# Streaming the split weights of `mm3` through TensorE from the last column to the first

## The chip, the cores and the metric

The kernel runs on one core of a Trainium2 chip. The metric is the device time of one execution in microseconds. The kernel before took 1279.71 us (median of two runs, 1278.69 and 1280.73).

## What is computed

Two blocks, one after the other, on x of 256 tokens by 1024 channels, all in float32. The first has a state space layer (S5) and an attention layer; the second has two layers, each with a mixing part of three branches (latent attention, convolution, retention) and a gated feed-forward part. Nearly all of the arithmetic is products of the activations with weight matrices of 1024 rows or so:

```python
def second_block(x, ...):
    for l in range(DEPTH):                       # DEPTH = 2, D_MODEL = 1024, SEQ = 256
        h = rms_norm_2(x, ln_mix_pre[l])
        proj = h @ w_in[l]                       # 1024 x 7584
        ...
        merged = gates[:, :, 0] * y_mla + gates[:, :, 1] * y_conv + gates[:, :, 2] * y_ret
        x = x + rms_norm_2(merged @ w_out[l], ln_mix_post[l])
        h = rms_norm_2(x, ln_ffn_pre[l])
        f = (jax.nn.silu(h @ ffn_w_gate[l]) * (h @ ffn_w_up[l])) @ ffn_w_down[l]
        x = x + rms_norm_2(f, ln_ffn_post[l])
    return x
```

## The kernel before, in words

Activations are held transposed, 128 channels of 256 tokens a block, and weights are streamed. A float32 operand is split into two of the type float32r, hi and lo, with hi + lo the operand; a product is then three matmuls, hi by hi, hi by lo and lo by hi, added up in one accumulator in PSUM.

`wtile` (L142) brings one tile of weights: SyncE's queue issues the DMA to `raw` (L149), 256 rows by 512 columns as 128 partitions of 2 x 512; ScalarE copies it to `hi` (L158, rounding it), VectorE subtracts to get `lo` (L160). Each of raw, hi and lo has four buffers in turn, and hi and lo two more from the second layer on, so how far loads and splits run ahead depends on when TensorE is done with a tile.

`mm3` (L163) issues the three matmuls of one accumulator and one block of 128 rows, L165, L166 and L167. The stationary operand is a block of the activations, 128 channels by 128 tokens, and the moving one is 128 rows of the tile of weights, as many columns as the tile has. [...] Nobody else calls these lines: `gemm` (L169) goes over the rows of a weight matrix two blocks of 128 at a time, and for each over the two halves of the tokens; `out_rows` (L241) does the same over 1024 output columns and adds the residual. What `gemm` has accumulated is read by the caller's `evac`, on ScalarE or VectorE. Between two tiles `pump` issues smaller work that is queued up: transposes, attention heads, taps of the convolution.

Other products don't go through `mm3`. `gemm_t` (L439; its matmuls are L454 to L456) has the weights stationary and 256 tokens moving, split as above. `gemm_raw` (L415; L428) does the same on float32 operands that are not split. Both serve the first layer, ahead of 165 us. Transposes (L203 and others) are matmuls by a unit matrix.

Each engine's instructions stand in the order in which the code issues them, which for the queued work is where `pump` takes it; semaphore waits are put in by the language's own tracking of tiles.

Of the kernel before, what the change touches and what calls it, by code (L numbers as in the profile page):

```python
# [9 lines left out]
F32 = mybir.dt.float32  # L10
# [5 lines left out]
PSUM = bass.MemoryType.PSUM  # L16
# [7 lines left out]
C = 512  # L24
# [26 lines left out]
class Net:  # L51
# [16 lines left out]
    def stage(self, pages, temps, raws=0, halves=0):  # L68
        """pages and temporaries of a stage; what an earlier stage had is given back."""
        if getattr(self, "ctx0", None):  # L70
            self.ctx0.close()
        self.ctx0 = ExitStack()
        self.temps = temps
        self.wn, self.more = {}, {"raw": raws, "hi": halves, "lo": halves}
        self.bp = self.ctx0.enter_context(self.tc.tile_pool(name=self.nm("bp"), bufs=pages))
        self.sp = self.ctx0.enter_context(self.tc.tile_pool(name=self.nm("sp"), bufs=2))
# [8 lines left out]
    def page(self, shape, name, dt=F32):  # L85
        """up to 4 KB of each partition"""
        assert int(np.prod(shape[1:])) <= 1024, shape
        return self.bp.tile(shape, dt, tag="q4", name=self.nm(name))
# [46 lines left out]
    def wbuf(self, tag):  # L135
        """buffer of a tile of weights; the stage may have some more of them"""
        i = self.wn[tag] = self.wn.get(tag, -1) + 1
        more = self.more.get(tag, 0)
        pool, bufs = (self.wp, 4) if i % (4 + more) < 4 else (self.sp, more)
        return pool.tile([128, KT, C], F32 if tag == "raw" else F32R, tag=tag, name=self.nm(tag), bufs=bufs)  # L140
# [22 lines left out]
    def mm3(self, out, xh, xl, wh, wl, first, last):  # L163
        nc = self.nc
        nc.tensor.matmul(out, xh, wh, start=first, stop=False)  # L165
        nc.tensor.matmul(out, xh, wl, start=False, stop=False)  # L166
        nc.tensor.matmul(out, xl, wh, start=False, stop=last)  # L167

    def gemm(self, xs, W, c0, ncols, evac, pts=None):  # L169
        """rows: out[t] = x @ W[:, c0:c0+ncols]; xs: list over k blocks of (hi, lo) aps [128, 256]."""  # L170
        KB = len(xs)
        pts = [self.acc(), self.acc()]
        for k0 in range(0, KB, KT):
            kn = min(KT, KB - k0)
            hi, lo = self.wtile(W[k0 * 128:(k0 + kn) * 128, c0:c0 + ncols], kn, ncols)
            for t in range(2):
                for k in range(kn):
                    xh, xl = xs[k0 + k]
                    s = slice(t * 128, t * 128 + 128)
                    self.mm3(pts[t][:, :ncols], xh[:, s], xl[:, s], hi[:, k, :ncols], lo[:, k, :ncols],  # L180
                             k0 + k == 0, k0 + k == KB - 1)
            self.pump()
        for t in range(2):
            evac(t, pts[t][:, :ncols])

    def split(self, dh, dl, src, scale=None):
        """dh + dl = src * scale, src in PSUM."""
        nc = self.nc
        if scale is None:
            nc.scalar.activation(dh, src, AF.Copy)  # L190
            nc.vector.tensor_tensor(dl, src, dh.bitcast(F32), op=ALU.subtract)
        else:
            a = nc.scalar.activation(dh, src, AF.Copy if isinstance(scale, float) else AF.Identity, scale=scale)  # L193
            self.last_split = a, nc.vector.scalar_tensor_tensor(dl, src, scale, dh.bitcast(F32), op0=ALU.mult, op1=ALU.subtract)  # L194

    def transposed(self, t, row, pages, nb, gains=None, scale=None):
        """row [128 tok, nb*128] -> split blocks of pages, scaled per channel by gains."""
        nc = self.nc
        for b0 in range(0, nb, 4):
            bn = min(4, nb - b0)  # L200
            pt = self.small()
            for b in range(bn):
                nc.tensor.transpose(pt[:, b * 128:(b + 1) * 128], row[:, (b0 + b) * 128:(b0 + b + 1) * 128], self.ident)  # L203
            s = slice(t * 128, t * 128 + 128)
            dh, dl = pages[b0 // 4]
            if gains is None:
                self.split(dh[:, :bn, s], dl[:, :bn, s],
                           pt[:, :bn * 128].rearrange("p (b n) -> p b n", b=bn), scale)
            else:
                for b in range(bn):  # L210
                    self.split(dh[:, b, s], dl[:, b, s], pt[:, b * 128:(b + 1) * 128],
                               gains[:, b0 + b:b0 + b + 1])
# [28 lines left out]
    def out_rows(self, xs, W, x, post, out=None):  # L241
        """x + rms(xs @ W) * post, or x + xs @ W when post is None; the first 128 rows are done some tiles ahead."""
        nc = self.nc
        KB = len(xs)
# [47 lines left out]
    def rsqrt1(self, v):  # L292
        """-1024 / 27 / sqrt(v) of a column, by a step of third and one of second order."""
# [16 lines left out]
    # ------------------------------------------------------------------ consts  # L310
# [25 lines left out]
    def sincos(self, out_c, out_s, ang, tag, after=None):  # L336
        """sin and cos of ang (any size that float32 reduces), ang [128, ...]"""
# [18 lines left out]
    def tables2(self):  # L356
# [8 lines left out]
        self.cs = self.sp.tile([128, 2, 2, 80], F32, tag="cs", name="cs", bufs=1)  # (cos/sin, t, mla16|ret64)  # L365
# [5 lines left out]
        # log gammas: min(x, 0) - log1p(exp(-|x|)), log1p by the atanh series  # L371
# [20 lines left out]
        # distances: [m part, mt, n]: relu(n - m), relu(m - n)  # L392
# [9 lines left out]
    # ------------------------------------------------------------------ first block: state space layer  # L402
    def raw_tiles(self, W, c0, ncols, KB):
        """sources of the tiles of gemm_raw, in its order"""
        return [W[k0 * 128:(k0 + KT) * 128, c0 + n0:c0 + n0 + C] for k0 in range(0, KB, KT) for n0 in range(0, ncols, C)]

    def load_raw(self):
        """next tile of self.todo, in any of the buffers of a tile of weights"""
# [6 lines left out]
    def gemm_raw(self, xs, ncols, evac, after=None):  # L415
        """gemm_t on float32 operands that are not split, where the tensor engine has the time: a closure for each tile of self.pre."""
# [22 lines left out]
    def gemm_t(self, xs, W, c0, ncols, evac, order=None):  # L439
        """columns: out^T = W[:, c0:c0+ncols]^T x^T, evac(block, psum [128, 256]); order of the pairs of k blocks."""  # L440
# [20 lines left out]
    def s5_params(self, after):  # L461
# [10 lines left out]
        # powers of ab: [ri, pair, k], k = 0..4  # L472
# [18 lines left out]
        # one chunk further, on (re, -im): [[a, b], [-b, a]] of ab^4  # L491
# [5 lines left out]
        # f = (ab - 1) / (lr + i li)  # L497
# [15 lines left out]
        # sums for products in three multiplications  # L513
# [4 lines left out]
    def s5_bc(self):  # L518
# [4 lines left out]
        # B~ = f B  # L523
# [20 lines left out]
    def s5_pows(self):  # L544
        """powers 1..16 of ab^4: (-im, re, im), pair, power."""
# [19 lines left out]
    def cprod(self, eng, q, l0, Z, Zx):  # L565
        """ab^l z for pairs 8q..8q+7, l = l0..l0+3, as (k1, k2, k3): re = k1 + k3, im = k1 + k2."""
# [14 lines left out]
    def s5_w(self, q, eng):  # L581
        """pairs 8q..8q+7 of ab^k B~, k = 1..4, [(g2, p), qq, (q2, k, c)], pair = 2 qq + q2, re and im."""
# [7 lines left out]
    def s5_wt(self, W, q, w, after=None):  # L590
        """their lhsT [(q2, k, c), qq, (g2, p)]"""
# [8 lines left out]
    def s5_c(self, cab, q, eng):  # L600
        """pairs 8q..8q+7 of [(g2, p), pair, (l, c')] of C ab^l, l = 0..3, re and im."""
# [4 lines left out]
    def s5(self, x_in):  # L606
# [6 lines left out]
        # normalised input; gains go on its channels after the transposes  # L613
# [6 lines left out]
        # gains go on the channels of the input; 1 / rms on what comes out of the first product and on what goes into the second  # L620
# [47 lines left out]
        # block diagonal B~ (re, -im) and the zeros before the kernel taps  # L668
# [55 lines left out]
        # chunk inputs X = W u: [(g2, p), (re, -im), pair, 1 + j], replaced by the states after each chunk  # L724
# [14 lines left out]
        # scan over the 64 chunks: inside 4 groups of 16, across the groups, then what each group takes over  # L739
# [28 lines left out]
        # kernel taps K[l] = Re(C ab^l B~): [(q4, g2, c), pg, (l, c')], channels in order; spread to lower triangles  # L768
# [19 lines left out]
        # inside a chunk  # L788
# [58 lines left out]
        # gated linear unit, output  # L847
# [25 lines left out]
    # ------------------------------------------------------------------ second block: mixing  # L873
    def mix(self, l, x):
# [11 lines left out]
        # ---- gates, branch outputs, merge  # L886
# [31 lines left out]
    def conv(self, l, xs, W, hf):  # L918
        """a * sigmoid(gate), taps, layer norm over channels and silu; the taps are left to run beside what follows."""
# [80 lines left out]
    def rope_rows(self, o1, o2, x1, x2, c, s, tag):  # L1000
        """o1 = x1 c - x2 s, o2 = x2 c + x1 s"""
# [42 lines left out]
    def mla(self, l, parts):  # L1044
        """latent attention; its rows and heads are left to run beside what follows."""
# [102 lines left out]
    def retention(self, l, xs, W, rstd, half, gn):  # L1148
# [41 lines left out]
        def score(h):  # L1190
            """scores on their decay, D^T[m, n] = gamma_f^(n - m) or gamma_b^(m - n)"""
# [54 lines left out]
    # ------------------------------------------------------------------ first block: causal attention  # L1246
# [128 lines left out]
    # ------------------------------------------------------------------ ffn  # L1375
# [25 lines left out]
def _cols(a, w):  # L1401
    """[..., w*128] -> [128, n*w]: one column per block of 128 channels."""
# [68 lines left out]
```

## Time and profile before

| | |
|---|---|
| time, median of two runs | 1279.71 us |
| span of the profiled execution, first to last instruction | 1276.7 us |
| TensorE busy | 1235.7 us, 97% |
| VectorE busy | 948.3 us, 74% |
| ScalarE busy | 652.9 us, 51% |
| DMA | 210.6 MB, mean 165 GB/s |

The profiled execution's own time is given as its span alone, which lies 3.0 us below the median of the runs. Busy time is the time in which an engine had an instruction under way; matmuls overlap each other, so the distance of their starts and not their durations tells how fast they go. A line of a group names the tile that is written, an arrow, and the tiles that are read.

### The profile page before, as it was taken

To read this page: it belongs to the slowest core of one execution; us is meant where nothing else is said; L and a number is where in the kernel's file an instruction comes from. 1 tells how busy PE (TensorE), PEld (TensorE's weight loads), DVE (VectorE), ACT (ScalarE), POOL (GpSimd) and SP (SyncE) were. 2 spreads that over 40 slices of the span, in tenths; PEclk is the share of its full clock that TensorE was granted. 3 is DMA by queue.
4 is the path that set the end of the run, shared out by engine and by line. 5 is a ranking of instruction groups with operands and counts; after the bars stand their busy time and mean duration, and the time that the engine had idled before them with its cause. 6 is when DMAs were issued, how large, how long until landed. Compare 5 with 4: busy or idle time off the path is not lost.

```text
span 1276.7 us, 17877 instructions
## 1 busy us (share of the span) xinstructions
PE 1235.7 (97%) x6520; PEld 1029.5 (81%) x6520; DVE 948.3 (74%) x1923; ACT 652.9 (51%) x1073; POOL 51.8 (4%) x42
## 2 busy tenths in 40 slices
PE   7898799999999999999999999999999999999997
PEld 6787777787888888888788887888888887888886
DVE  6999489887889998857755555899998857755544
ACT  3112467675765544544644444666545445644432
POOL 3920000000000000000000000000000000000000
PEclk9779899999999999999999999999999999999999
DMA  9326656644454554555566564544554554665661
GB/s 319 83 43 99 166 174 209 192 136 137 142 164 138 161 161 152 164 201 179 189 180 184 171 235 151 175 134 147 166 159 153 179 184 148 218 190 161 193 211 50
DMA packets 125367, 210.60 MB, mean 165 GB/s; under 512 B 22112, under 2 KB 31328, under 8 KB 125280
## 3 DMA queue, kind: packets, MB, share of 16 engines
q1 hardware_dynamic: 117056, 204.24, 50.9%
q10 hardware_dynamic: 8224, 5.23, 2.1%
q8 instruction: 51, 0.84, 0.3%
q14 instruction: 36, 0.29, 0.1%
HBM read 205.83 MB, written 3.60 MB: 164 GB/s over the span
## 4 chain that ended last, share of the span: by engine, by line
PE 79%; DVE 13%; ACT 3%; DMA 3%; issue 2%; SPq 0%; DVEq 0%; ACTq 0%
PE mm L165 23%; PE mm L167 23%; PE mm L166 22%; DVE lo L160 2%; PE sm L203 2%; ACT hi L158 1%; PE sm L1119 1%; PE sm L1211 1%; DVE cacc L957 1%; PE sm L1094 1%; DVE s5pr L745 1%; PE sm L733 1%; DVE cm L586 1%; DVE s5pr L759 1%; PE mm L455 1%
## 5 line engine op out<-in xcount | busy, mean ns | idle before, releaser
L160 DVE TENSOR_TENSOR lo<-raw,hi 128x1024 fp32r<-128x1024 f32 (+2 forms) x372 | 440.1, 1186 | 235.8 <-ACT hi L158 234.4
L158 ACT ACTIVATE hi<-raw 128x1024 fp32r<-128x1024 f32 (+2 forms) x372 | 382.6, 1032 | 377.8 <-PE mm L167 290.4
L165 PE MATMUL mm<-hi,xTh 128*128 128x512 f32 (+2 forms) x1152 | 451.1, 394 | 1.6 <-ACT xTh L193 1.5
L167 PE MATMUL mm<-hi,xTl 128*128 128x512 f32 (+2 forms) x1152 | 443.7, 386 | 0.3 <-DVE t L297 0.2
L166 PE MATMUL mm<-lo,xTh 128*128 128x512 f32 (+2 forms) x1152 | 443.3, 385 | 0.2 <-DVE lo L160 0.2
L165 PEld LDWEIGHTS mm<-hi,xTh 128*128 128x128 f32 x1152 | 216.4, 188 | 48.9 <-ACT xTh L193 7.3
L167 PEld LDWEIGHTS mm<-hi,xTl 128*128 128x128 f32 x1152 | 216.3, 188 | 46.2 <-DVE t L297 1.5
L166 PEld LDWEIGHTS mm<-lo,xTh 128*128 128x128 f32 x1152 | 216.7, 188 | 41.2 <-DVE lo L160 0.5
L957 DVE SCALAR_TENSOR_TENSOR cacc<-aT,colp,cacc 128x256 f32<-128x256 f32 x240 | 104.2, 476 | 0.0
L165 PE MATMUL mm<-hi,fh 128*128 128x512 f32 x176 | 69.0, 392 | 0.0
L166 PE MATMUL mm<-lo,fh 128*128 128x512 f32 x176 | 68.9, 392 | 0.0
L167 PE MATMUL mm<-hi,fl 128*128 128x512 f32 x176 | 68.8, 391 | 0.0
L167 PEld LDWEIGHTS mm<-hi,fl 128*128 128x128 f32 x176 | 33.0, 187 | 7.4
L165 PEld LDWEIGHTS mm<-hi,fh 128*128 128x128 f32 x176 | 33.0, 188 | 7.3
L166 PEld LDWEIGHTS mm<-lo,fh 128*128 128x128 f32 x176 | 33.0, 188 | 7.2
L277 DVE SCALAR_TENSOR_TENSOR pg<-mm,post 128x512 f32<-128x512 f32 x16 | 11.0, 690 | 21.9 <-ACT pg L275 21.9
L194 DVE SCALAR_TENSOR_TENSOR xTl<-sm,colp,xTh 128x128 fp32r<-128x128 f32 x80 | 24.3, 345 | 3.5 <-ACT xTh L193 3.1
L454 PE MATMUL mm<-s5gh,hi 128*128 128x256 f32 x64 | 19.0, 305 | 7.1 <-ACT s5gh L844 7.1
L193 ACT ACTIVATE xTh<-sm,colp 128x128 fp32r<-128x128 f32 x80 | 24.4, 381 | 1.8 <-DVE xTl L194 1.7
L895 ACT ACTIVATE pg<-mm,t 128x512 f32<-128x512 f32 x24 | 16.5, 690 | 16.9 <-PE mm L167 16.9
L733 PE MATMUL sm<-s5U,s5W 64*64 64x64 f32 x256 | 21.2, 300 | 2.5 <-DMA s5U<-s5ud 2.5
L733 PEld LDWEIGHTS sm<-s5U,s5W 64*64 64x64 f32 x256 | 20.8, 207 | 3.2 <-issue 3.2
(387 smaller groups left out, 1513.2 us busy)
## 6 DMA issues: line engine op xcount, KB each, us to landing
raw<-in_w_in SPq DMA_DIRECT2D x112, 512.0 KB, 3.5
raw<-in_ffn_w_down SPq DMA_DIRECT2D x44, 512.0 KB, 3.8
raw<-in_ffn_w_gate SPq DMA_DIRECT2D x40, 512.0 KB, 3.7
raw<-in_ffn_w_up SPq DMA_DIRECT2D x40, 512.0 KB, 3.6
raw<-in_attn_w_in SPq DMA_DIRECT2D x32, 512.0 KB, 4.3
raw<-in_ret_w_o SPq DMA_DIRECT2D x16, 512.0 KB, 3.2
raw<-in_w_out SPq DMA_DIRECT2D x16, 512.0 KB, 3.2
raw<-in_ssm_w_glu SPq DMA_DIRECT2D x8, 512.0 KB, 4.9
```

The costliest lines, as they stand in the source:

```text
L158: nc.scalar.activation(h, r, AF.Copy)
L160: self.last_lo = nc.vector.tensor_tensor(l, r, h.bitcast(F32), op=ALU.subtract)
L165: nc.tensor.matmul(out, xh, wh, start=first, stop=False)
L166: nc.tensor.matmul(out, xh, wl, start=False, stop=False)
L167: nc.tensor.matmul(out, xl, wh, start=False, stop=last)
L193: a = nc.scalar.activation(dh, src, AF.Copy if isinstance(scale, float) else AF.Identity, scale=scale)
L194: self.last_split = a, nc.vector.scalar_tensor_tensor(dl, src, scale, dh.bitcast(F32), op0=ALU.mult, op1=ALU.subtract)
L203: nc.tensor.transpose(pt[:, b * 128:(b + 1) * 128], row[:, (b0 + b) * 128:(b0 + b + 1) * 128], self.ident)
L454: nc.tensor.matmul(o, wh, xh, start=first and b % 2 == 0, stop=False, skip_group_check=True)
L733: lx[q] = nc.tensor.matmul(pt[g * 64:g * 64 + 64, qq * 64:qq * 64 + 64], Wl[i][h][r, qq, g * 64:g * 64 + 64], U[r, 8 * h + qq, g, :], star ...
L895: nc.scalar.activation(gate[t, n], p, AF.Tanh, scale=hf(t))
L957: nc.vector.scalar_tensor_tensor(cacc[:, b, :], src, sc, cacc[:, b, :], op0=ALU.mult, op1=ALU.add)
```

## The change

In `mm3` three views are turned round in the free dimension: the output, and the hi and the lo half of the weights. A step of 1 from column 0 becomes a step of -1 from the last column. The activations, which are stationary, are as before. Docstrings and comments are taken out as well, without effect on the program; the matmuls' lines become L166, L167 and L168.

```diff
     def mm3(self, out, xh, xl, wh, wl, first, last):
         nc = self.nc
+        out, wh, wl = out[:, ::-1], wh[:, ::-1], wl[:, ::-1]
         nc.tensor.matmul(out, xh, wh, start=first, stop=False)
         nc.tensor.matmul(out, xh, wl, start=False, stop=False)
         nc.tensor.matmul(out, xl, wh, start=False, stop=last)
```

No instruction changes its place on any engine. What differs in the order is waits, 90 on TensorE and two on VectorE. On TensorE, in the attention layer's product, where `mm_2755` and `mm_2756` are the accumulators of the two halves of the tokens, `hi_2758` and `lo_2759` the tile of weights, `xTh_1802` and `xTl_1803` the activations, `sm_2521` and `sm_2552` the scores of two heads, and a name with _49 a semaphore of an engine, this stands before:

```order
L165 MATMUL mm_2755<-hi_2758,xTh_1802 128x512
L166 MATMUL mm_2755<-lo_2759,xTh_1802 128x512
L167 MATMUL mm_2755<-hi_2758,xTl_1803 128x512
L165 MATMUL mm_2756<-hi_2758,xTh_1802 128x512 [waits Activation_49]
L1303 MATMUL sm_2521<-akT_1886,aqT_1884 128x256 [waits Activation_49]
L1304 MATMUL sm_2521<-akT_1886,aqT_1884 128x128
L1303 MATMUL sm_2552<-akT_1886,aqT_1884 128x256 [waits PE_49]
```

And this on TensorE at the same place of the changed kernel:

```order
L166 MATMUL mm_2755<-hi_2758,xTh_1802 128x512
L167 MATMUL mm_2755<-lo_2759,xTh_1802 128x512
L168 MATMUL mm_2755<-hi_2758,xTl_1803 128x512
L166 MATMUL mm_2756<-hi_2758,xTh_1802 128x512 [waits PE_49,Activation_49]
L1304 MATMUL sm_2521<-akT_1886,aqT_1884 128x256 [waits Activation_49]
L1305 MATMUL sm_2521<-akT_1886,aqT_1884 128x128
L1304 MATMUL sm_2552<-akT_1886,aqT_1884 128x256
```

The wait on TensorE's own semaphore has gone from the second head's scores to the first matmul of the accumulator `mm_2756`. Over the whole program 52 matmuls of L165, each the first of an accumulator, have such a wait more, and 38 matmuls of other lines have one less. VectorE's split to lo loses a wait on TensorE at two tiles.

## Rows read from the trace of the kernel before

**Rows 1.** From the page: span, TensorE's busy share, its busy digits and granted clock in 40 slices, and the chain of work that ended last, by engine and by line.

```profile
span 1276.7 us, 17877 instructions
PE 1235.7 (97%) x6520; PEld 1029.5 (81%) x6520; DVE 948.3 (74%) x1923; ACT 652.9 (51%) x1073; POOL 51.8 (4%) x42
PE   7898799999999999999999999999999999999997
PEclk9779899999999999999999999999999999999999
PE 79%; DVE 13%; ACT 3%; DMA 3%; issue 2%; SPq 0%; DVEq 0%; ACTq 0%
PE mm L165 23%; PE mm L167 23%; PE mm L166 22%; DVE lo L160 2%; PE sm L203 2%; ACT hi L158 1%; PE sm L1119 1%; PE sm L1211 1%; DVE cacc L957 1%; PE sm L1094 1%; DVE s5pr L745 1%; PE sm L733 1%; DVE cm L586 1%; DVE s5pr L759 1%; PE mm L455 1%
```

**Rows 2.** Who waited for whom, in total, with the number of times and the longest: TensorE's longest and those of `mm3`, and the longest of the other engines' that bears on the weights.

```profile
PE mm L454 <- ACT s5gh L844: 7.1, 1, 7.1
PE sm L597 <- DVE cm L586: 6.4, 4, 3.2
PE sm L638 <- DMA first<-in_c_first: 5.0, 1, 5.0
...
PE mm L165 <- ACT xTh L193: 1.5, 6, 0.3
...
ACT hi L158 <- PE mm L167: 290.4, 194, 3.5
```

**Rows 3.** Groups of instructions of line L165, kept apart by shape (partitions x columns of the output): count, busy time in us, mean ns of one, idle time before them.

```profile
L165 PE MATMUL mm<-hi,xTh 128*128 128x512 f32 x1056 | 421.9, 401 | 1.1 <-ACT xTh L193 1.0
L165 PE MATMUL mm<-hi,fh 128*128 128x512 f32 x176 | 69.0, 392 | 0.0
L165 PE MATMUL mm<-hi,xTh 128*128 128x256 f32 x64 | 18.1, 284 | 0.0
L165 PE MATMUL mm<-hi,oTh 128*128 128x512 f32 x32 | 13.1, 410 | 0.0
L165 PE MATMUL mm<-hi,s5mh 128*128 128x512 f32 x32 | 12.8, 403 | 0.1
L165 PE MATMUL mm<-hi,cTh 128*128 128x512 f32 x32 | 12.7, 397 | 0.0
L165 PE MATMUL mm<-hi,xTh 128*128 128x416 f32 x32 | 11.6, 380 | 0.6 <-ACT xTh L193 0.5
L165 PE MATMUL mm<-hi,mcTh 128*128 128x512 f32 x16 | 6.3, 391 | 0.0
L165 PE MATMUL mm<-hi,mcTh 128*128 128x256 f32 x8 | 2.2, 279 | 0.0
```

**Rows 4.** TensorE's instructions in order of time from 839.7 us on: start in us, duration in us, line, output and operands.

```profile
839.71 0.39 PE L166 MATMUL mm<-lo,xTh 128*128 128x512 f32 x1
839.94 0.39 PE L167 MATMUL mm<-hi,xTl 128*128 128x512 f32 x1
840.17 0.39 PE L165 MATMUL mm<-hi,xTh 128*128 128x512 f32 x1
...
841.57 0.39 PE L165 MATMUL mm<-hi,xTh 128*128 128x512 f32 x1
841.80 0.39 PE L166 MATMUL mm<-lo,xTh 128*128 128x512 f32 x1
```

**Rows 5.** Busy time of each engine in three stretches, and behind POOL's the clock granted to TensorE, the DMA share and GB/s.

```profile
91.00:97.00 6.00, 6.00 (x29) 5.30 (x28) 6.00 (x23) 0.00 (x0) 4.28 (x1) 1.00 0.20 66
142.00:145.00 3.00, 3.00 (x16) 3.00 (x15) 0.00 (x0) 1.56 (x2) 0.00 (x0) 0.50 0.96 292
840.00:845.00 5.00, 5.00 (x23) 4.03 (x22) 5.00 (x17) 4.24 (x8) 0.00 (x0) 1.00 0.00 0
```

**Rows 6.** The waits of line L165 that take an instruction of their own in the weight-loading queue: durations in ns (least, median, longest), first and last start.

```profile
L165 PEldq EVENT_SEMAPHORE  x26: 51/51/51, 190.0 to 1028.1; - x26
```

**Rows 7.** TensorE in order of time from 142 us on, the matmuls of `gemm_t` on 256 columns.

```profile
142.05 0.41 PE L456 MATMUL mm<-s5gh,lo 128*128 128x256 f32 x1
142.27 0.41 PE L454 MATMUL mm<-s5gh,hi 128*128 128x256 f32 x1
142.48 0.41 PE L455 MATMUL mm<-s5gl,hi 128*128 128x256 f32 x1
142.69 0.41 PE L456 MATMUL mm<-s5gh,lo 128*128 128x256 f32 x1
```

**Rows 8.** TensorE in order of time from 92 us on, the matmuls of `gemm_raw`, runs of the same group merged: start of the first, time to the end of the last, count.

```profile
92.06 3.62 PE L428 MATMUL mm<-s5x,lo 128*128 128x256 f32 x16
95.51 3.62 PE L428 MATMUL mm<-s5x,raw 128*128 128x256 f32 x16
```

**Rows 9.** TensorE in order of time at 190 us, where `mm3` begins behind transposes.

```profile
190.34 0.49 PE L203 MATMUL sm<-first,x 128*128 128x128 f32 x3
190.60 0.47 PE L165 MATMUL mm<-hi,xTh 128*128 128x512 f32 x1
190.91 0.39 PE L166 MATMUL mm<-lo,xTh 128*128 128x512 f32 x1
```

## The prediction

> **What bounds the kernel now.** I read the page's busy times and clock line first, then its chain of work [rows 1]. TensorE is busy 97% of a 1276.7 us span, and from the sixth of 40 slices on the digits of its busy share are nines but for the last; those of its granted clock are nines from the sixth on. The chain that ended last is TensorE for 79%, and 68% of it is the three lines of `mm3`, L165 to L167. So the time of this kernel is, to first order, the number of columns that TensorE streams times the time for one.
>
> Second, the list of who waited for whom on TensorE [rows 2]: its longest waits are 7.1, 6.4 and 5.0 us, once or a few times each, on lines of the first block. Waits of `mm3` (L165) are 1.5 us together. The other way round, ScalarE's split of the weights (L158) waits 290 us for the last matmul of a tile (L167): the weights are ready before TensorE wants them, and the engines that make them wait for buffers. Nothing but TensorE's own pace is worth time behind `mm3`.
>
> Third, how many matmuls the change touches, from the groups kept apart by shape [rows 3]. L165 issues 1056 + 176 + 32 + 32 + 32 + 16 = 1344 of 512 columns, 64 + 8 = 72 of 256 and 32 of 416; L166 and L167 issue as many. That is 4032, 216 and 96: 4344 matmuls, 4032 x 512 + 216 x 256 + 96 x 416 = 2.160 million columns.
>
> Fourth, the pace of one. The durations of the groups (some 390 ns) overlap, so they are no price; the starts are. In a stretch of nothing but `mm3` ten starts, nine steps, lie within 2.09 us [rows 4], 232 ns for 512 columns, 0.454 ns each. [...] Each 10% on that price is 98 us: only this price matters.
>
> **The change, part by part.** Moved: nothing. Each engine's instructions stand in the order of before, DMAs and SP's queue included; the three matmul lines only stand one line lower. The view on the moving operand and that on the PSUM output now run from the last column to the first; the stationary operand (128 columns of x) is as it was. Since both are turned, each result lies where it lay, so no reader on ScalarE or VectorE changes and none is late or early by itself.
>
> Added: waits of TensorE on its own earlier matmuls. Fifty-two first matmuls of an accumulator get one, thirty-eight other matmuls lose one, as the two lists of the change show. All that are waited for stand ten or more matmuls back in TensorE's own order. Ten at even 100 ns are 1 us, and a matmul's duration is 0.39 us [rows 4], so they are done when the wait is reached. Where a matmul has two waits, the second takes an instruction of its own in the queue, 51 ns in the trace [rows 6]; sixteen more of these are 0.8 us if nothing hides them, and they run ahead in the loading queue, beside a matmul of 232 ns. I take 0; bounds 0 and 0.8 us. VectorE loses two waits at L160: 0, since it waits for ScalarE there.
>
> Turned: 4344 matmuls read and write downwards. No row of before has such a matmul, so its price is bounded from the nearest rows. [...] At a granted clock of 0.50 [rows 5] matmuls of 256 columns start every 213 ns [rows 7], 0.833 ns a column; at a clock of 1.00 [rows 5] those whose float32 operands are not split (L428) take 3.45 us for 16 [rows 8], 216 ns for 256 columns, 0.842 ns. The cost would be 2.160 million x (0.833 - 0.454) = 819 us, by L428's price 838 us.
>
> Between ends so far apart I take the row that the instruction is nearest to: the same operand types, the same 4-byte step, the same tile, the same clock, which is rows 4, and a price of 0. What speaks for it is what the stream has to do at 0.454 ns: consecutive columns are fetched from, and put into, neighbouring words, and neighbours stay neighbours when the order is turned. The sum is 0 to 0.8 us on 1276.7 us. The profiled span lies 3.0 us below the median of 1279.7 us shown; the same difference gives a forecast of 1280 us.
>
> [...]
>
> **The rivals.**
> [...]
>
> A start-up gap: turned operands keep up within a matmul, but each begins anew instead of running on from the one before. Where `mm3` begins behind another kind of matmul the next start comes after 310 ns [rows 9] in place of 232, some 80 ns more. Over 4344 matmuls that is 348 us: 1628 us; half or double of the gap gives 1454 to 1976 us. Against it: the gap in those rows follows a change of operation, and the stretch of rows 4 changes its tile of weights with no gap at all.
>
> [...]
>
> That the change does not do what it says (both views turned back into one upward stream when the program is built) would look like the forecast, and shares its chance.
>
> **How the numbers follow.** No cost 0.62, with a range of its own from 1270 to 1295 us; half rate 0.24, 2099 to 2118 us; start-up gap 0.12, 1454 to 1976 us; faster 0.02, from 1199 us. The no-cost case has the largest chance, so the time is 1280 us. The first and the third hold only 0.74, so the range has to reach the half-rate rival: 1268 to 2120 us. A measurement of this kernel tells about 2% from no change. Slower by over 2% is half rate and gap, 0.36; within 2% the forecast, 0.62; faster 0.02.
>
> **What would show it.** Right: in the stretch of rows 4, nine steps in 2.0 to 2.2 us, now on L166 to L168; TensorE 97% busy; the waits of L158 on the last matmul near 290 us; TensorE's new waits nowhere among its idle time. [...] Wrong by a gap: the same excess in ns on 256 as on 512 columns. A span over 1305 us with rows 4's pace kept would mean that the waits, taken at 0, cost something.

## The result, and the profile after

The changed kernel took 1291.29 us (median of two runs, 1290.32 to 1292.26) beside 1279.71 us before: a ratio of 1.0091, 95% interval 1.0062 to 1.0121. It is 11.6 us slower: within the 2% that the forecast called no change, clear of the noise, and not the nothing that the sum had. The profiled execution's span went from 1276.7 to 1290.1 us, by 13.4 us.

From the page of the changed kernel, in the order of [rows 1]: span, busy time, TensorE's digits, granted clock, and the chain that ended last.

```profile
span 1290.1 us, 17871 instructions
PE 1249.0 (97%) x6520; PEld 1031.2 (80%) x6520; DVE 949.3 (74%) x1923; ACT 653.4 (51%) x1073; POOL 51.9 (4%) x42
PE   7898799999999999999999999999999999999997
PEclk9778899999999999999999999999999999999999
PE 81%; DVE 12%; ACT 3%; DMA 2%; issue 2%; SPq 0%; DVEq 0%; ACTq 0%
PE mm L166 23%; PE mm L167 23%; PE mm L168 23%; PE sm L204 2%; DVE lo L160 1%; PE sm L1120 1%; PE sm L1212 1%; DVE cacc L958 1%; PE sm L1095 1%; ACT hi L158 1%; DVE s5pr L746 1%; PE sm L734 1%; DVE cm L587 1%; DVE s5pr L760 1%; DVE cm L575 1%
```

TensorE is busy 13.3 us longer, nearly the whole of it, at the same share and, in all but one of the 40 slices, the same clock; VectorE's and ScalarE's busy times are within 1 us of before. So neither a new wait nor another engine took the time. The list of waits says the same; it answers to [rows 2], columns as there.

```profile
PE mm L455 <- ACT s5gh L845: 7.8, 1, 7.8
PE sm L598 <- DVE cm L587: 6.4, 4, 3.2
PE sm L819 <- DVE s5X L763: 5.4, 1, 5.4
...
PE mm L166 <- ACT xTh L194: 1.4, 6, 0.3
```

The first three lie in the first block. `mm3` waits 1.4 us in place of 1.5, and ScalarE's split of the weights (L158) waits 300.8 us for the last matmul of a tile in place of 290.4. The waits of TensorE on itself have come in, as instructions of their own on L166, 44 in place of 26 [rows 6], and none of them stands among the idle times:

```profile
L166 PEldq EVENT_SEMAPHORE  x44: 51/51/199, 191.0 to 1223.2; - x44
```

What has grown is the matmul itself. The largest group, to be read against the first of [rows 3], is at a mean of 406 ns in place of 401; the same tile with lo is at 398, in place of 393:

```profile
L166 PE MATMUL mm<-hi,xTh 128*128 128x512 f32 x1056 | 427.1, 406 | 1.0 <-ACT xTh L194 0.9
L167 PE MATMUL mm<-lo,xTh 128*128 128x512 f32 x1056 | 420.5, 398 | 0.0
```

A mean hides how. In the stretch of [rows 4], from one matmul earlier on and in order of time after (start, duration), nine steps take 2.10 us, 233 ns each, as against 2.09 us:

```profile
847.90 0.40 PE L166 MATMUL mm<-hi,xTh 128*128 128x512 f32 x1
848.14 0.40 PE L167 MATMUL mm<-lo,xTh 128*128 128x512 f32 x1
...
850.00 0.40 PE L166 MATMUL mm<-hi,xTh 128*128 128x512 f32 x1
```

But some 20 us earlier there is a stretch of before in which 45 steps take 10.19 us, 226 ns each (first and last start of it):

```profile
815.73 0.39 PE L165 MATMUL mm<-hi,xTh 128*128 128x512 f32 x1
815.95 0.39 PE L166 MATMUL mm<-lo,xTh 128*128 128x512 f32 x1
...
825.92 0.39 PE L165 MATMUL mm<-hi,xTh 128*128 128x512 f32 x1
```

The same 46 matmuls after take 10.50 us, 233 ns a step:

```profile
823.78 0.40 PE L166 MATMUL mm<-hi,xTh 128*128 128x512 f32 x1
824.02 0.40 PE L167 MATMUL mm<-lo,xTh 128*128 128x512 f32 x1
...
834.28 0.40 PE L166 MATMUL mm<-hi,xTh 128*128 128x512 f32 x1
```

The granted clock of this stretch before (behind POOL's busy time) is the 1.00 of [rows 5]:

```profile
816.00:825.00 9.00, 9.00 (x41) 7.46 (x40) 8.40 (x30) 7.21 (x15) 0.00 (x0) 1.00 0.58 186
```

So before had two paces, some 227 and 233 ns for the same instruction at the same clock, and the change has one. To see what divides them I put beside each matmul of the trace the address of its operands in SBUF, where the tiles lie, from the built program. It is the buffer of the weights. `hi` and `lo` have four buffers each that exist all along (addresses 35200 to 67968, "low") and two more from the second layer on (190016 to 206400, "high"). Summed over the whole trace, from each `mm3` matmul of 512 columns to the next start, steps that are over 245 ns in either trace kept apart as gaps:

| | count | before, us | after, us | difference, us |
|---|---|---|---|---|
| low buffers | 2590 | 590.7 | 604.6 | +13.9 |
| high buffers | 1276 | 297.7 | 297.9 | +0.2 |
| gaps, both | 165 | 58.3 | 57.6 | -0.7 |

The matmuls of 416 and 256 columns differ by 0.2 us together. Nearly all of the 13.4 us is 2590 matmuls of the low buffers, which went from 228 to 233.4 ns; those of the high buffers were at 233 before.

### The profile page after: what moved, and what is told of

Its sections match the earlier page's. It is cut to its first block, busy times and chain, and to the rows that moved or that the text cites. A ratio compares the mean times of both kernels' runs of the same rounds, so it can differ in the third digit from the quotient of the medians.

```text
span 1290.1 us, 17871 instructions
## 1 busy us (share of the span) xinstructions
PE 1249.0 (97%) x6520; PEld 1031.2 (80%) x6520; DVE 949.3 (74%) x1923; ACT 653.4 (51%) x1073; POOL 51.9 (4%) x42
## 4 chain that ended last, share of the span: by engine, by line
PE 81%; DVE 12%; ACT 3%; DMA 2%; issue 2%; SPq 0%; DVEq 0%; ACTq 0%
PE mm L166 23%; PE mm L167 23%; PE mm L168 23%; PE sm L204 2%; DVE lo L160 1%; PE sm L1120 1%; PE sm L1212 1%; DVE cacc L958 1%; PE sm L1095 1%; ACT hi L158 1%; DVE s5pr L746 1%; PE sm L734 1%; DVE cm L587 1%; DVE s5pr L760 1%; DVE cm L575 1%
## 5 line engine op out<-in xcount | busy, mean ns | idle before, releaser
L158 ACT ACTIVATE hi<-raw 128x1024 fp32r<-128x1024 f32 (+2 forms) x372 | 382.7, 1032 | 388.3 <-PE mm L168 300.8
L166 PE MATMUL mm<-hi,xTh 128*128 128x512 f32 (+2 forms) x1152 | 456.5, 398 | 1.6 <-ACT xTh L194 1.4
L168 PE MATMUL mm<-hi,xTl 128*128 128x512 f32 (+2 forms) x1152 | 449.4, 391 | 0.3
L167 PE MATMUL mm<-lo,xTh 128*128 128x512 f32 (+2 forms) x1152 | 449.4, 391 | 0.1
L166 PEld LDWEIGHTS mm<-hi,xTh 128*128 128x128 f32 x1152 | 216.7, 188 | 51.9 <-ACT xTh L194 7.2
L168 PEld LDWEIGHTS mm<-hi,xTl 128*128 128x128 f32 x1152 | 216.6, 188 | 49.3 <-DVE t L298 1.5
L167 PEld LDWEIGHTS mm<-lo,xTh 128*128 128x128 f32 x1152 | 216.9, 188 | 44.3 <-DVE lo L160 0.4
L166 PE MATMUL mm<-hi,fh 128*128 128x512 f32 x176 | 70.0, 398 | 0.0
L168 PE MATMUL mm<-hi,fl 128*128 128x512 f32 x176 | 69.9, 397 | 0.0
L167 PE MATMUL mm<-lo,fh 128*128 128x512 f32 x176 | 69.9, 397 | 0.0
L168 PEld LDWEIGHTS mm<-hi,fl 128*128 128x128 f32 x176 | 33.1, 188 | 8.1
L167 PEld LDWEIGHTS mm<-lo,fh 128*128 128x128 f32 x176 | 33.1, 188 | 7.8
L166 PEld LDWEIGHTS mm<-hi,fh 128*128 128x128 f32 x176 | 33.1, 188 | 7.8
```

What stands on the lines that cost most here:

```text
L158: nc.scalar.activation(h, r, AF.Copy)
```

## The experiments

Two questions were open: does reading the weights downwards or writing PSUM downwards cost (or the waits), and why did before have two paces. In the twelve runs, "step" is the mean distance of the starts of two 512-column matmuls in a row, gaps over 245 ns left out. "Up" and "down" are the order of the columns.

**e_read**: the changed kernel with the weights alone turned.

```diff
-        out, wh, wl = out[:, ::-1], wh[:, ::-1], wl[:, ::-1]
+        wh, wl = wh[:, ::-1], wl[:, ::-1]
```

Expected:

> Only the weights are read from the last column to the first; the accumulators are written upwards, so the columns of each product come out in reverse order. In the two traces the 13.4 us of the whole change lie in the step from one 512-column matmul to the next: 227 ns in most of before, 233 ns everywhere in the change. Theory 1, reading: what costs is where the stream of weights begins in SBUF (the first column read lies at byte 124 or 60 of a 128-byte line, in place of 0 or 64): steps of 233 ns in all buffers, 1291 us. Theory 2, writing: downward writes to PSUM cost: steps of 227 ns in the four low buffers as before, 1280 us. Theory 3, the 14 more waits of TensorE on itself (this kernel has 93 of them, like before): 1280 us.

Measured: 1292.47 us, ratio to before 1.0107 (1.0093 to 1.0120). Steps of 233.4 ns in low and in high buffers; the largest group has the mean of the whole change:

```profile
L166 PE MATMUL mm<-hi,xTh 128*128 128x512 f32 x1056 | 427.1, 406 | 1.0 <-ACT xTh L194 0.9
```

**e_write**: the accumulators alone.

```diff
-        out, wh, wl = out[:, ::-1], wh[:, ::-1], wl[:, ::-1]
+        out = out[:, ::-1]
```

Expected:

> Only the accumulators are written from the last column to the first; the weights are read upwards, so the columns of each product come out in reverse order. It has the 107 waits of TensorE on itself that the whole change has. Theory 1, reading: steps of 227 ns in the four low buffers, 1280 us. Theory 2, writing: 233 ns everywhere, 1291 us. Theory 3, waits: 1291 us with steps of 227 ns and longer ones at the waits alone.

Measured: 1278.29 us, ratio 0.9998 (0.9989 to 1.0006). Steps of 227.9 ns low and 233.3 ns high, and the group is at the 401 ns of before [rows 3]:

```profile
L166 PE MATMUL mm<-hi,xTh 128*128 128x512 f32 x1056 | 421.8, 401 | 1.1 <-ACT xTh L194 1.0
```

These two settle the first question. All of the cost is in reading (ratio 1.0107, low buffers at 233.4 ns); writing PSUM from the last column to the first costs nothing that can be measured (0.9998, low buffers at 227.9 ns), and neither do the 14 more waits, which e_write has too.

**f_pad64** and **f_halves**: why two paces. Both start from the kernel before. The first has a 64-byte tile ahead of all others:

```diff
+        nc.gpsimd.memset(self.cp.tile([128, 16], F32, name="pad"), 0.0)
         first = self.cp.tile([128, 232], F32, name="first")
```

> The kernel before, both views upwards, with a tile of 64 bytes ahead of all others, so that every tile lies 64 bytes higher: the weights in the four low buffers (hi and lo) start at byte 64 of a 128-byte line in place of 0, those in the two high ones at 0 in place of 64. Before had 227 ns in the low buffers and 233 ns in the high ones. If the place in the line decides, they change sides: 233 ns low, 227 ns high, about 2700 matmuls up and 1330 down by 5 to 6 ns, +7 us, 1287 us. If the address region decides (low buffers near 35 to 68 thousand, high ones near 190 to 206 thousand), or the place of the weights against that of the activations (which move along), the low ones keep 227 ns, 1280 us.

Measured: 1279.65 us, ratio 1.0007 (0.9998 to 1.0016); low 227.9, high 233.3 ns, as before. The place within 128 bytes by itself decides nothing (the low buffers start at byte 64 in place of 0 and keep their pace): that theory fell.

The second has a small tile just ahead of the two high buffers 64 bytes larger, at two places in the code (one is shown, cut short):

```diff
-        rsum = self.sp.tile([128, 2, 8], F32, tag="m_sum", ...)
+        rsum = self.sp.tile([128, 2, 16], F32, tag="m_sum", ...)
```

> The kernel before, both views upwards, with one small tile ahead of the two high buffers made 64 bytes larger, so that these start at byte 0 of a 128-byte line, as the low ones do; nothing else that TensorE reads moves. If the place in the line decides, or that against the activations: 227 ns in all buffers, some 1330 matmuls faster by 5 to 6 ns, 7 us less, 1273 us. If the address region decides: 233 ns stay in the high buffers, 1280 us.

Measured: 1272.31 us, ratio 0.9950 (0.9937 to 0.9962): it beats both kernels. 227.6 ns in the low and in the high buffers, and the matmuls of [rows 4], the same ones, now take 2.04 us for nine steps, 1.81 us for the eight shown here:

```profile
836.54 0.39 PE L166 MATMUL mm<-lo,xTh 128*128 128x512 f32 x1
836.77 0.39 PE L167 MATMUL mm<-hi,xTl 128*128 128x512 f32 x1
...
838.35 0.39 PE L165 MATMUL mm<-hi,xTh 128*128 128x512 f32 x1
```

The address region is out as well, since these buffers lie where they lay but for 64 bytes and went from 233.3 to 227.6 ns. So is another engine's access to SBUF: steps during which VectorE, ScalarE and GpSimd had nothing under way are at 227.2 ns in the low buffers and 233.3 ns in the high ones before (71 and 64 steps), and at 226.6 ns in the high ones of f_halves (38). What is left is the distance of the weights from the other operand that TensorE reads, the stationary activations.

**f_rel32, f_rel96, f_rel128**: that distance varied, upwards, by a tile of 32, 96 or 128 bytes between the low buffers and everything behind them (the first is shown).

```diff
         self.wp = pool("wp", 4)
+        self.pd = pool("pd", 1)
...
+        nc.gpsimd.memset(self.pd.tile([128, 8], F32, name="pad"), 0.0)
```

> The runs so far: 233 ns come from reading downwards, not from writing; and upwards the weights go at 227 ns where they and the stationary activations start at the same byte of a 128-byte line (0 and 0, or 64 and 64), at 233 ns where they start 64 bytes apart. Here, upwards, a 32-byte tile between the weights' low buffers and everything behind them moves the activations: low buffers start at 0 against 32, high ones at 96 against 32 (64 apart, as before). If only the same byte goes at 227: low buffers 233 ns, 1292 us. If it is enough to lie in the same 64-byte half: 227 ns low, 1279 us. The high ones stay at 233 ns either way.

> Upwards, the activations 96 bytes further against the low buffers, so that the weights start 32 bytes behind them within a 128-byte line: the distance not seen yet, after 0 (227 ns), 64 and 96 (233 ns). Theory place, only distance 0 is fast: 233 ns in all buffers, 1292 us. Rival, one of the four quarters is as good: 227 ns low, 1279 us.

> Upwards, the activations 128 bytes further against the low buffers: the same byte of a 128-byte line, but no longer of a 256-byte one. If the place within 128 bytes decides: 227 ns low, 233 ns high, as before, 1279 us. If a longer stretch decides: 233 ns in all, 1292 us.

Measured: f_rel32 1291.19 us, ratio 1.0099 (1.0084 to 1.0114); f_rel96 1294.22 us, 1.0121 (1.0108 to 1.0135); f_rel128 1287.81 us, 1.0081 (1.0068 to 1.0093). The low buffers went to 233.1, 234.1 and 232.5 ns. At a distance of 32 bytes the group, at 404 ns, is nearly where turning put it:

```profile
L166 PE MATMUL mm<-hi,xTh 128*128 128x512 f32 x1056 | 425.5, 404 | 1.0 <-ACT xTh L194 0.9
```

So an upward stream loses as much by a shift of its neighbour (233.1 ns, f_rel32) as by turning (233.4 ns). Of f_rel128's two cases the second came true: the same byte of 128 is not enough, the same of 256 is what all the 227 ns have in common. A longer stretch is not needed: f_halves has the low buffers at 0 and the high ones at 256 bytes modulo 512 from the activations, and 227.6 ns in both.

**f_plus4, r_plus4**: hi and lo one element further in their buffers, upwards and downwards. The buffers are also 128 bytes longer, so every second one lies 128 bytes further off on top of the 4 that the expectations name.

```diff
-        return pool.tile([128, KT, C], ...)
+        t = pool.tile([128, KT * C + 32], F32R, tag=tag, name=self.nm(tag), bufs=bufs)
+        return t[:, 1:1 + KT * C].rearrange("p (k c) -> p k c", k=KT)
```

> Upwards, hi and lo one element further in their buffers (which are 128 bytes longer): low buffers start at byte 4 against 0 of the activations, high ones at 68 against 0. If only the same byte goes at 227: 233 ns low, 1292 us. If the same 64-byte half is enough: 227 ns low, 1279 us. [...]

> The changed kernel (downwards) with hi and lo one element further: the first column read now starts at byte 0 of a 128-byte line in the low buffers, as upwards, and at 64 in the high ones; in the change it was 124 and 60. Theory direction: a downward stream of 512 columns takes 233 ns wherever it starts: 1291 us. Theory place of the first column: 227 ns in the low buffers, 1278 us.

Measured: f_plus4 1306.64 us, ratio 1.0225 (1.0209 to 1.0240), steps of 237.9 ns low and 237.7 ns high; r_plus4 1299.04 us, 1.0161 (1.0146 to 1.0176), 235.6 ns in both. Against the same distance without the 4 bytes, where the table below has it, that is 4 to 9 ns more upwards and 2 ns more downwards. The group of f_plus4 is the longest of all:

```profile
L168 PE MATMUL mm<-hi,xTh 128*128 128x512 f32 x1056 | 430.7, 409 | 0.9 <-ACT xTh L196 0.8
```

Neither 233 nor 227 ns came out in f_plus4's low buffers: the 4 bytes cost by themselves, 237.1 ns at a distance of 4 beside 228.0 at 0 before. Of r_plus4's two theories neither came true. In half of its low tiles the first column read lies where an upward stream starts that goes at 227 ns, at distance 0, and these go at 235.7 ns: the place of the first column is not it.

**r_rel32, r_rel96, r_halves**: the layouts of f_rel32, f_rel96 and f_halves with the three views turned.

> The changed kernel (downwards) with the activations 32 bytes further against the low buffers: first column at 124 against activations from 32 on, in the high ones at 92 against 32. Theory direction: 233 ns in all buffers, 1291 us. Theory that downwards, too, some place against the activations is faster (32 apart is the one not seen yet, after 0 and 64): 227 ns in some buffers, 1278 to 1285 us.

> Downwards, the same layout as f_rel96, the last of the four distances (0, 64 and 96 gave 233 ns downwards). Theory direction: 233 ns in all buffers, 1291 to 1292 us. Rival, this is the downward stream's own fast place: 227 ns low, 1278 us.

> The changed kernel (downwards) with the small tile of f_halves made 64 bytes larger, so that all twelve buffers of hi and lo lie at the same byte of a 128-byte line as the activations. Upwards this layout had 227 ns in all buffers and 1272.3 us. Theory place: downwards a 512-column stream takes 233 ns wherever it lies, so nothing moves against the change, 1291 us, and turning costs 19 us in this layout in place of 12. Rival, turning adds about the same 3 ns to each matmul whatever its place: 1284 to 1286 us.

Measured: 1292.39 us, ratio 1.0115 (1.0099 to 1.0132); 1291.09 us, 1.0101 (1.0086 to 1.0117); 1291.44 us, 1.0101 (1.0088 to 1.0115). Steps of 233.3 to 233.4 ns in every buffer of each. r_halves is the sharpest of them: in this layout turning costs 1291.4 - 1272.3 = 19.1 us, as expected from the place and not the 12 to 14 us of a fixed price per matmul. Its group is again where the change has it:

```profile
L166 PE MATMUL mm<-hi,xTh 128*128 128x512 f32 x1056 | 427.4, 406 | 1.0 <-ACT xTh L194 0.9
```

All steps side by side. Distance is the address of the first element of the weights' tile less that of the activations, modulo 256, that is, what is left after whole multiples of 256 bytes; 224 is 32 bytes short of a multiple, 192 is 64 short and 160 is 96 short:

| | columns read | low: distance, step ns | high: distance, step ns | time us |
|---|---|---|---|---|
| before | up | 0, 228.0 | 192, 233.3 | 1279.7 |
| e_write | up | 0, 227.9 | 192, 233.3 | 1278.3 |
| f_pad64 | up | 0, 227.9 | 192, 233.3 | 1279.7 |
| f_halves | up | 0, 227.6 | 0, 227.6 | 1272.3 |
| f_rel128 | up | 128, 232.5 | 192, 233.2 | 1287.8 |
| f_rel32 | up | 224, 233.1 | 192, 233.3 | 1291.2 |
| f_rel96 | up | 160, 234.1 | 192, 233.3 | 1294.2 |
| f_plus4 | up | 4, 237.1 and 132, 238.8 | 196, 237.8 and 68, 237.7 | 1306.6 |
| after | down | 0, 233.4 | 192, 233.4 | 1291.3 |
| e_read | down | 0, 233.4 | 192, 233.4 | 1292.5 |
| r_halves | down | 0, 233.4 | 0, 233.4 | 1291.4 |
| r_rel32 | down | 224, 233.4 | 192, 233.4 | 1292.4 |
| r_rel96 | down | 160, 233.3 | 192, 233.4 | 1291.1 |
| r_plus4 | down | 4, 235.7 and 132, 235.6 | 196, 235.6 and 68, 235.7 | 1299.0 |

## Why the prediction was right, and where it was not

**What bounds the kernel** held: the time is `mm3`'s columns times TensorE's pace. A change of 5.4 ns on 2590 matmuls, 13.9 us, came out in the span as 13.4 us, with nothing to hide it.

**Moved and added: 0** held. The waits cost nothing that can be measured (e_write, 0.9998), and the longest waits for the accumulators, ScalarE's in `out_rows`, come to 26.6 us together in place of 25.9.

**Turned: a price of 0** was the step that failed, by its size. It cost 3.3 ns on the mean of the 4032 matmuls of 512 columns (13.9 us, less 0.7 us of shorter gaps), against an upper bound of 194 ns a matmul. Two links in it were wrong. The pace of 232 ns was read in one stretch, and as it happens in the high buffers; the two thirds of the matmuls that were at 227 ns, the ones with something to lose, were not seen, though the starts of the trace before show them. And "neighbours stay neighbours" looked at the stream of weights alone, where the pace also depends on how it lies to the activations (228.0 ns at a distance of 0 before, 233.1 at 224 in f_rel32). That the time stayed within the forecast's own range of 1270 to 1295 us is owed to the size of the loss, 2% of a matmul. No step of the prediction bounded it there, so the closeness of 1280 us is in part luck.

**Half rate**, the 0.833 ns a column that [rows 7] has at a granted clock of 0.50 and so 427 ns for 512 columns, did not come: 233 ns, at a granted clock of 1.00 in this stretch (behind POOL's busy time):

```profile
824.00:833.00 9.00, 9.00 (x40) 7.26 (x39) 8.15 (x30) 6.71 (x14) 0.00 (x0) 1.00 0.65 199
```

One of its two prices, that of L428, was misread. The 16 matmuls of [rows 8] are two records for each of the eight that `gemm_raw` issues for a tile, so a matmul of unsplit float32 operands takes 431 ns for 256 columns (3.45 us for eight), not 216. No run shows a matmul of `mm3` near either price: the longest mean step is 238.8 ns for 512 columns, in f_plus4.

**A start-up gap** was too large as a size, 80 ns. Of its kind (the same excess on 256 as on 512 columns) there is nothing either: matmuls of 256 columns in the low buffers go from 120.4 to 119.4 ns, and in the high ones from 114.1 to 117.7. The prediction's argument against it, that the stretch of [rows 4] changes its tile of weights without a gap, does not stand on these rows: the ten matmuls shown read one tile. The next tile begins at 842.27 us, with no gap indeed, 0.23 us behind the matmul at 842.04.

**Faster**, from 1199 us, did not come either. That time rests on an estimate of 0.417 ns a column, half of those 0.833 ns, which no run shows: the shortest mean step of 512 columns is 227.6 ns, 0.445 ns each, upwards in f_halves (1272.31 us), and downwards none is below 233.3 ns. What there was to gain, 6 ns, lay upwards in the other third of the matmuls, and f_halves gained it.

What stays open is the mechanism inside TensorE. That the distance to the activations decides is shown upwards by f_halves, f_pad64 and the three f_rel runs (227.6 to 228.0 ns at 0, 232.5 to 234.1 elsewhere): TensorE loads a stationary operand while a matmul streams (weight loads are under way in 81% of the span, beside matmuls in 97% [rows 1]), and nothing else that it reads in `mm3` was moved against the weights. That the load has a part in the step is inferred from this by elimination alone; no run shows it. That downwards no distance helps is shown for four of them (0, 160, 192 and 224; 233.3 to 233.4 ns) and for four more that are 4 bytes off (235.6 to 235.7 ns); 128 was not tried. Why the distance matters, and whether a turned stationary operand would give the 227 ns back downwards, was not tried.

## What to carry to other kernels

Where TensorE is the bound, read its pace as the distance of the starts, for each buffer of its operands and not in one stretch: the same instruction can have two (228.0 and 233.3 ns in the kernel before). A moving operand may be read from its last column to its first and an accumulator written so without a large cost (ratio 1.0091), but the read gives up what a good layout gives: here 6 ns of 233 on each matmul of 512 columns. Put the tiles of streamed weights at the same byte of 256 as the stationary tiles where the matmuls have 512 columns: 64 bytes of padding were worth 0.5% of this kernel (f_halves). At 256 columns it was the other way round (below).

## What the runs showed of the hardware that was not expected

- The step of a matmul of 512 float32r columns, read upwards, by 128 activations depends on the distance of its two operands in SBUF, 227.6 ns at 0 modulo 256 and 232.5 to 234.1 ns at 32, 64, 96 or 128 from that. In f_rel32 only that distance was changed of all that the matmuls of the low buffers read, and the step grew from 228.0 to 233.1 ns. That the load of the activations has a part in it was not shown.
- At 256 columns the sign was the other one. Matmuls of 256 columns in the kernel before go at 120.4 ns in the low buffers and at 114.1 ns in the high ones, and f_halves brought the high ones to 119.6. At 32, 96 and 128 bytes (f_rel32, f_rel96, f_rel128) the low ones are at 119.3, 118.9 and 119.9.
- A start 4 bytes off costs some 10 ns upwards against the best place (237.1 to 238.8 beside 227.6) and 2 ns downwards (235.6 beside 233.4).
- Writing PSUM downwards cost nothing: 1278.29 us beside 1278.95 us of the kernel before on the same chip.
